# The experts' weight loads wait for a free part of the ring alone, no longer for the load two places before

## The chip, the cores and the metric

The kernel runs on one core of one Trainium2 chip. The metric is the device time of one execution in microseconds, over several executions of the same program; lower is better.

## The reference

Two blocks are computed on 512 tokens of width 1024, in float32. The first is a gated delta rule with a convolution module, followed by a mixture of experts; the second is a diagonal state-space mixer with a convolution, followed by a squared-ReLU MLP. The change touches the mixture of experts alone:

```python
N_EXPERTS = 64; TOP_K = 6; D_EXPERT = 256
scores = jax.nn.sigmoid((hf @ router_w).astype(jnp.float32))
...
_, top_idx = lax.top_k(jnp.where(exp_keep, sel, -jnp.inf), TOP_K)
...
def swiglu(h, wg, wu, wd):
    return (jax.nn.silu(h @ wg) * (h @ wu)) @ wd
def expert_block(args):
    tok, e = args
    return swiglu(h_pad[tok], w_gate[e], w_up[e], w_down[e])
```

Each token goes to 6 of 64 experts. One expert's weights (gate and up 1024 x 256 each, down 256 x 1024) are 3 MB in float32; all 64 are needed in each execution.

## The kernel before, in words

The program is written in a tile framework: each engine has its own stream of instructions, and the framework adds the semaphore waits that the use of tiles demands. Loads are issued by SP (SyncE), whose queue is in order: a transfer that waits holds up all that SP issues behind it.

The experts run as 42 blocks (`BLOCKS`, from `plan`, L1072). Four fixed experts have one block each; the other sixty are ranked by how many tokens they got, and the block of a rank is known when the program is built, while the expert of that rank is read from a table on the chip (`eid`) into a register of SP. A block has up to 128 rows of tokens and belongs to one expert, to two (64 rows each) or to four (32 rows each). Blocks with one expert and blocks with several take turns; the busiest ranks need two blocks, of which the second finds its weights already there.

For each block `blocks` (L1641) does the following. `load_block` asks for the weights: three parts of 1 MB for each expert (part 0 and 1 are gate and up for the first and second half of the 1024 inputs, part 2 is down), all parts 0 first, then all parts 1, then all parts 2. Each part goes into the next slot of a ring (`slot`, L1186): ten slots of their own (`RING`), two more in the memory of `x1` (tag `ewx1`) from the third block on, and in their place three older ones from the 18th block's end on (`free_first`); for the last six blocks (`LEAVE`) ten again. A load must wait until PE has done the last matmul that reads the slot's former content. `rows_ahead` lets POOL (GpSimd) gather the rows of a later block from `hrow` in HBM into one of three tiles X. `ffn` (L1597) turns the rows on PE (`pt_xb`), scales them on DVE and ACT (`xTb`), multiplies by gate and up (`gub`), applies SiLU on ACT (`sgb`) and the product on DVE (`hb`), turns again (`pt_hb`), and multiplies by down (`pyb`) in two halves, which DVE brings into one of three tiles `y`. `scatter` (L1633) lets POOL add the rows to one of two accumulators in HBM (`yacc`), in turn; two scatter-adds on the same accumulator follow one another, each waiting for the one before to land. The gathers and scatter-adds together are called rows below; they go through POOL's DMA queue (q0), the loads through SP's (q1).

In `load` (L1501), the list `order` holds the issued loads. From the third load on, each gets a dependency on the load two places before it (`FLIGHT = 2`, L1061), so that it is issued only when that one has landed. A second, different dependency on `order[-8]` concerns the order of register reads in the program and is no wait for data.

Between the blocks PE also computes the shared expert (`shared`, `shared_out`, at `HID` and `OUT`, behind blocks 10 to 16). Behind block 17 (`SECOND`) the memory of the first stage is given back and SP loads `row_g_final`, `sbc` and `ssd` for the second block. Behind the last expert block, SP issues the first `w_in` loads of the second block, and `beyond` (L1670) waits for all scatter-adds; then `block_two` reads both accumulators (`sums`).

Of the kernel before, what the change touches and what calls it, by code (L numbers as in the profile page):

```python
# [200 lines left out]
class ModWeights:  # L201
# [10 lines left out]
    def load(self):  # L212
        if self.todo:
            j, q = self.todo.pop(0)
            tag, bufs = self.slots[self.n % len(self.slots)]
            self.n += 1
            r = self.rows
            w = self.k.W.tile([P, r, 512], F32, tag=tag, name=f"wm{j}_{q}", bufs=bufs)
            self.k.nc.sync.dma_start(w, self.k.I["w_mod"][j, :, q * r:q * r + r, :])
            self.have.append(w)  # L220
# [837 lines left out]
        50, 49, 46, 45, 44, 44, 43, 42, 41, 41, 40, 39, 38, 37, 37, 32, 32, 32, 31, 30, 30, 28, 26, 25, 23, 22, 20, 20, 18, 17, 16]  # L1058
CAPS = [-(-c // 16) * 16 for c in CAPS]
NOV = 72  # L1060
FLIGHT = 2  # L1061
LEAVE = 6
LAST = 0
AHEAD = 2
# [82 lines left out]
class Moe:  # L1147
# [353 lines left out]
    def load(self, who):  # L1501

        k, nc = self.k, self.k.nc
        if who in self.wt:
            return self.wt[who]
        kind, r = who
        if kind == "rank":
            ins, (v,) = nc.values_load_multi_w_load_instructions(self.eid[:, r:r + 1], engines=[mybir.EngineType.SP],
                                                                 min_val=0, max_val=NE - 1)
            if len(self.order) >= 8:  # L1510
                for q in ins:
                    k.tc.add_manual_dep(q.ins, self.order[-8].ins.name,
                                        mybir.DependencyInfo(mybir.DependencyClass.NoSync, mybir.DependencyReason.DATA),
                                        reason="few registers at a time")
            src = k.I["ew"][bass.ds(v, 1)].rearrange("a p f -> p (a f)")
        else:
            src = k.I["sw"] if kind == "shared" else k.I["ew"][r]
        ts = []

        def part(i):  # L1520
            t = self.slot(f"ew{kind}{r}_{i}")
            q = nc.sync.dma_start(t, src[:, 2048 * i:2048 * i + 2048])
            if len(self.order) >= FLIGHT:
                k.tc.add_manual_dep(q.ins, self.order[-FLIGHT].ins.name,
                                    mybir.DependencyInfo(mybir.DependencyClass.Sync, mybir.DependencyReason.DATA),
                                    reason="few loads in flight, for the rows' sake")
            self.order.append(q)
            ts.append(t)
        self.wt[who] = (ts, part)
        return self.wt[who]  # L1530
# [949 lines left out]
```

## Time and profile before

| | us |
|---|---|
| median of 3 runs (2093.59 to 2098.49) | 2096.74 |
| the profiled execution, its own time | 2084.69 |
| its span, first to last instruction | 2082.9 |
| PE busy | 1853.8 (89%) |
| DVE busy | 994.3 (48%) |
| ACT busy | 596.6 (29%) |
| POOL busy | 501.8 (24%) |

In the profile, times are microseconds (us) from the start of the span unless marked ns. PE is TensorE's matmuls, PEld its weight loads, DVE VectorE, ACT ScalarE, POOL GpSimd, SP SyncE; SPq is SP's queue of issues. L1522 is line 1522 of the kernel; all matmuls stand under one helper's line (L139), so they are told apart by the tile that they write (`gub`, `pyb`, `pt_xb`). A digit of the slices is the busy share in tenths. PEclk is the granted clock of TensorE as a share of full speed. The DMA share is the mean busy share of the core's 16 DMA engines and can pass 1 where packets overlap. A transfer's landing is counted from its issue. An engine's wait is put down to what ended it last.

### The profile page before, as it was taken

To read this page: it belongs to the slowest core of one execution; us is meant where nothing else is said; L and a number is where in the kernel's file an instruction comes from. 1 tells how busy PE (TensorE), PEld (TensorE's weight loads), DVE (VectorE), ACT (ScalarE), POOL (GpSimd) and SP (SyncE) were. 2 spreads that over 40 slices of the span, in tenths; PEclk is the share of its full clock that TensorE was granted. 3 is DMA by queue.
4 is the path that set the end of the run, shared out by engine and by line. 5 is a ranking of instruction groups with operands and counts; after the bars stand their busy time and mean duration, and the time that the engine had idled before them with its cause. 6 is when DMAs were issued, how large, how long until landed. Compare 5 with 4: busy or idle time off the path is not lost. (4 is left out here: it accounts for less than half of the span.)

```text
span 2082.9 us, 24082 instructions
## 1 busy us (share of the span) xinstructions
PE 1853.8 (89%) x8465; PEld 1244.2 (60%) x8465; DVE 994.3 (48%) x2205; ACT 596.6 (29%) x1124; POOL 501.8 (24%) x408
## 2 busy tenths in 40 slices
PE   5997698987798898988888983999999999999998
PEld 3775476875653333333322321888888878888886
DVE  4789944668764211352211215677433453323352
ACT  5443321114332111111111112533333344323341
POOL 1315334533232221212111213543100112201300
PEclk9998888999889999999999997999999999999999
DMA  7354353226589999999999996333332333233241
GB/s 301 134 184 134 95 169 90 74 86 242 188 308 339 348 357 332 338 361 369 351 339 340 367 339 206 105 95 89 101 102 86 101 117 112 89 94 101 81 142 41
DMA packets 136001, 408.53 MB, mean 196 GB/s; under 512 B 43813, under 2 KB 56229, under 8 KB 109513
## 3 DMA queue, kind: packets, MB, share of 16 engines
q1 hardware_dynamic: 110040, 365.17, 49.8%
q0 software_dynamic: 12016, 40.25, 7.7%
q10 hardware_dynamic: 13824, 1.58, 0.5%
q8 instruction: 67, 1.10, 0.2%
q14 instruction: 54, 0.43, 0.1%
HBM read 365.13 MB, written 40.63 MB: 195 GB/s over the span
## 5 line engine op out<-in xcount | busy, mean ns | idle before, releaser
L139 PE MATMUL gub<-ewrank,xTb 128*64 128x512 f32 (+5 forms) x960 | 289.4, 625 | 28.1 <-DMA ewrank<-ew 27.8
L139 PEld LDWEIGHTS gub<-ewrank,xTb 128*64 128x64 f32 (+5 forms) x960 | 94.2, 146 | 199.4 <-issue 156.1
L274 DVE TENSOR_TENSOR wlo<-wraw,whi 128x1024 fp32r<-128x1024 f32 (+1 forms) x103 | 120.8, 1173 | 139.1 <-ACT whi L273 133.7
L273 ACT CAST whi<-wraw 128x1024 fp32r<-128x1024 f32 (+1 forms) x115 | 113.9, 990 | 212.2 <-PE psi L139 50.6
L139 PE MATMUL pyb<-ewrank,hTb 128*64 128x512 f32 (+5 forms) x440 | 155.5, 602 | 5.5 <-DMA ewrank<-ew 3.4
L1616 DVE SCALAR_TENSOR_TENSOR hb<-gub,tw,sgb 128x256 f32<-128x256 f32 (+5 forms) x38 | 18.3, 482 | 274.9 <-ACT sgb L1614 274.9
L139 PE MATMUL psi<-xnh,whi 128*128 128x512 f32 (+1 forms) x368 | 141.7, 386 | 0.0
L139 PE MATMUL psi<-xnl,whi 128*128 128x512 f32 (+1 forms) x368 | 141.4, 384 | 0.0
L1638 POOL DMA_INDIRECT yacc<-yb,tok x63 | 89.0, 1413 | 179.3 <-DVE yb L1630 132.9
L1338 ACT ACTIVATE xTb<-pt_xb,B,A 128x128 f32<-128x128 f32 (+5 forms) x168 | 74.1, 445 | 174.4 <-DVE xTb L1340 173.3
L1593 POOL DMA_INDIRECT X<-hrow,tok x38 | 36.9, 972 | 338.3 <-PE pt_xb L142 332.6
L139 PE MATMUL psi<-xnh,wlo 128*128 128x512 f32 (+1 forms) x296 | 113.3, 383 | 0.0
L1340 DVE TENSOR_SCALAR xTb<-pt_xb,A,B 128x128 f32<-128x128 f32 (+5 forms) x168 | 65.5, 392 | 88.0 <-PE pt_xb L142 51.7
L1614 ACT ACTIVATE sgb<-gub 128x256 f32<-128x256 f32 (+5 forms) x42 | 16.0, 382 | 315.4 <-PE gub L139 315.4
L2403 POOL TENSOR_TENSOR fr<-fr 128x512 f32<-128x512 f32 x32 | 48.7, 1522 | 238.1 <-ACT fr L2402 238.1
L139 PE MATMUL psf<-xml,whi 128*128 128x512 f32 (+1 forms) x272 | 102.5, 377 | 0.2 <-DVE xml L274 0.2
L139 PE MATMUL psf<-xmh,whi 128*128 128x512 f32 (+1 forms) x272 | 102.4, 377 | 0.2 <-ACT xmh L273 0.2
L139 PE MATMUL psf<-xmh,wlo 128*128 128x512 f32 (+1 forms) x272 | 102.4, 377 | 0.0
L139 PEld LDWEIGHTS pyb<-ewrank,hTb 128*64 128x64 f32 (+5 forms) x440 | 46.8, 141 | 78.9 <-issue 64.1
L1630 DVE TENSOR_TENSOR yb<-pyb,gt 128x512 f32<-128x512 f32 (+5 forms) x84 | 57.9, 690 | 71.7 <-PE pyb L139 70.1
L139 PEld LDWEIGHTS psi<-xnh,whi 128*128 128x128 f32 x368 | 69.7, 190 | 14.3 <-ACT xnh L2268 0.4
L139 PEld LDWEIGHTS psi<-xnl,whi 128*128 128x128 f32 x368 | 69.9, 190 | 13.5
(752 smaller groups left out, 4032.6 us busy)
## 6 DMA issues: line engine op xcount, KB each, us to landing
ewrank<-ew SPq DMA_DIRECT2D x168, 1024.0 KB, 7.1
wraw<-w_in SPq DMA_DIRECT2D x59, 512.0 KB, 3.6
wraw<-ff SPq DMA_DIRECT2D x32, 512.0 KB, 3.5
wf<-ff SPq DMA_DIRECT2D x64, 256.0 KB, 2.7
wm<-w_mod SPq DMA_DIRECT2D x28, 512.0 KB, 7.8
ewfix<-ew SPq DMA_DIRECT2D x12, 1024.0 KB, 5.7
ewx<-ew SPq DMA_DIRECT2D x12, 1024.0 KB, 6.9
wm<-w_mod SPq DMA_DIRECT2D x10, 1024.0 KB, 5.7
```

What stands on the lines that cost most here:

```text
L139: return self._done(self.eng.matmul(out, lhsT, rhs, **kw), rate, rhs)
L273: nc.scalar.copy(hi, raw)
L274: (eng or nc.vector).tensor_tensor(lo, raw, hi.bitcast(F32), ALU.subtract)
L1338: nc.scalar.activation(dst(c), pt[:, i, :], AF.Identity, scale=sa, bias=sb)
L1340: nc.vector.tensor_scalar(dst(c), pt[:, i, :], sa, sb, ALU.mult, ALU.add)
L1593: self.k.nc.gpsimd.indirect_dma_start(out=X[0:idx.shape[0]], out_offset=None, in_=self.hrow, in_offset=bass.IndirectOffsetOnAxis(ap=idx, a ...
L1614: nc.scalar.activation(sg[0:n], gu[0:n, 0:256], AF.Silu)
L1616: nc.vector.scalar_tensor_tensor(h[0:n], gu[0:n, 256:512], wslot[0:n], sg[0:n], ALU.mult, ALU.mult)
L1630: nc.vector.tensor_tensor(y[0:n, cs], py[0:n], self.gt2[0:n, cs], ALU.mult)
L1638: self.k.nc.gpsimd.indirect_dma_start(out=self.yacc[self.nsc % 2], out_offset=bass.IndirectOffsetOnAxis(ap=idx, axis=0), in_=y[a:a + n], i ...
L2403: nc.gpsimd.tensor_tensor(r, r, r, ALU.mult)
```

## The change

The constant `FLIGHT` and the dependency on the load two places before are taken out. A load keeps the other conditions: its place in SP's order, its register, and its slot. Nothing else is edited.

```diff
-FLIGHT = 2
 LEAVE = 6
 LAST = 0
 AHEAD = 2
@@ -1520,10 +1519,6 @@
         def part(i):
             t = self.slot(f"ew{kind}{r}_{i}")
             q = nc.sync.dma_start(t, src[:, 2048 * i:2048 * i + 2048])
-            if len(self.order) >= FLIGHT:
-                k.tc.add_manual_dep(q.ins, self.order[-FLIGHT].ins.name,
-                                    mybir.DependencyInfo(mybir.DependencyClass.Sync, mybir.DependencyReason.DATA),
-                                    reason="few loads in flight, for the rows' sake")
             self.order.append(q)
             ts.append(t)
         self.wt[who] = (ts, part)
```

## Rows read from the trace of the kernel before

**Rows 1.** The slices of the page: 40 equal parts of the span, 52 us each.

```profile
DMA  7354353226589999999999996333332333233241
GB/s 301 134 184 134 95 169 90 74 86 242 188 308 339 348 357 332 338 361 369 351 339 340 367 339 206 105 95 89 101 102 86 101 117 112 89 94 101 81 142 41
```

**Rows 2.** The chain that ended last: start us, us, what.

```profile
1270.20 4.86 DMA yacc<-yb,tok
...
1307.38 5.76 PE psi L139 x42
```

**Rows 3.** Waits of SP's queue, 777 to 1262 us: total us, times, longest us.

```profile
SPq L1522 <- DMA ewrank<-ew: 363.7, 128, 8.7
SPq L1522 <- DMA ewx<-ew: 14.5, 5, 3.3
SPq L1522 <- PE gub L139: 3.1, 12, 0.4
```

**Rows 4.** Waits of PE, 777 to 1262 us, same columns.

```profile
PE pt_hb L142 <- DVE hb L1616: 30.3, 29, 1.3
PE gub L139 <- DMA ewrank<-ew: 27.8, 17, 4.2
PE pyb L139 <- DMA ewrank<-ew: 1.9, 3, 1.1
```

**Rows 5.** Windows: PE, PEld, DVE, ACT, POOL busy, then PEclk, DMA share, GB/s.

```profile
8.00:34.00 26.00, 15.61 (x104) 7.73 (x104) 11.21 (x33) 17.30 (x30) 3.09 (x11) 1.00 1.03 420
650.00:777.00 127.00, 116.85 (x497) 45.48 (x499) 31.86 (x78) 20.80 (x51) 30.13 (x24) 1.00 1.00 349
760.00:767.00 7.00, 6.15 (x18) 2.23 (x19) 1.83 (x3) 0.51 (x2) 0.82 (x1) 1.00 0.96 348
777.00:1262.00 485.00, 422.15 (x1467) 154.02 (x1460) 125.62 (x330) 72.84 (x174) 93.01 (x74) 0.96 0.99 348
882.00:887.00 5.00, 3.68 (x13) 1.70 (x12) 3.79 (x13) 1.51 (x4) 0.00 (x0) 1.00 1.04 431
```

**Rows 6.** DMA, 777 to 1262 us: queues, then issues with count and median landing us.

```profile
q1 hardware_dynamic: 20259, 144.47, 78.0%
q0 software_dynamic: 7069, 24.18, 20.4%
...
ewrank<-ew SPq DMA_DIRECT2D x131, 1024.0 KB, 7.2
ewx<-ew SPq DMA_DIRECT2D x4, 1024.0 KB, 6.9
...
yacc<-yb,tok POOLq DMA_INDIRECT x48, 8.3
...
X<-hrow,tok POOLq DMA_INDIRECT x26, 6.9
```

**Rows 7.** Windows, same columns: a wait of PE and what follows.

```profile
1210.00:1215.00 5.00, 1.37 (x6) 0.34 (x6) 0.00 (x0) 0.00 (x0) 0.00 (x0) 0.85 1.01 321
1215.00:1220.00 5.00, 5.00 (x12) 1.30 (x13) 0.00 (x0) 0.00 (x0) 0.00 (x0) 0.50 0.89 316
```

**Rows 8.** Timeline of SP's issues, 0 to 16 us: start us, us, what.

```profile
2.59 2.50 SPq L295 DMA_DIRECT2D xt<-x  x4
5.14 10.02 SPq L219 DMA_DIRECT2D wm<-w_mod  x8
```

**Rows 9.** Timeline of SP's issues, 871 to 878 and 886 to 890 us.

```profile
872.60 0.37 SPq L1824 DMA_DIRECT2D sbc<-sbc  x1
...
874.89 2.65 SPq L1522 DMA_DIRECT2D ewrank<-ew  x2
...
886.80 2.71 SPq L1522 DMA_DIRECT2D ewrank<-ew  x2
```

**Rows 10.** POOL's timeline from 876 us, and the landing of what is issued in 872:878.

```profile
876.45 0.99 POOL L1593 DMA_INDIRECT X<-hrow,tok  x1 [0.32 <-PE pt_xb L142]
...
X<-hrow,tok POOLq DMA_INDIRECT x1, 7.7
```

## The prediction

> **What bounds the kernel now.** I read the slices of the page first, to find the stage that the edited lines feed; then the chain that ended last, to see what a shorter stage is worth; then, for that stage alone, the waits of SP's queue and of PE; then the rates of single stretches and the share of each DMA queue, because they price the change.
>
> The slices [rows 1] show one long stretch, from the 13th slice to the 24th (52 us each, so some 625 to 1250 us), where the DMA digit stands at 9 and the rate at 332 to 369 GB/s. It is the stretch in which `load` (L1501) brings 64 experts of 3 MB each. Behind it the rate falls to about 100 GB/s. The chain [rows 2] leaves this stage by the last scatter-add, issued at 1270.20, and from 1307.38 on it runs through the second block on PE. So whatever the expert stage loses comes off the whole, one for one.
>
> In 777 to 1262 us, the part in which the loads lead, SP waited 363.7 + 14.5 us for the landing of an earlier expert load, and 3.1 us for PE's gate/up to free a slot, never longer than 0.4 us [rows 3]. So the ring had room, and the wait that is to be removed is the one that held the loads back. PE on its side waited 27.8 + 1.9 us for expert weights; another 30.3 us are the step through DVE and ACT between gate/up and down, which no load shortens [rows 4].
>
> **What the two-load limit costs.** The question is whether two loads already keep the DMA engines full. The windows say: nearly, not quite [rows 5]. At 8 to 34 us, where 512 KB loads follow one another without such a limit, the chip moved 420 GB/s at a DMA share of 1.03; at 882 to 887 us, with two expert loads behind a queue of others, 431 at 1.04. At 760 to 767 us only expert loads, two at a time, were under way: 348 GB/s at 0.96. Over 777 to 1262 it was 348 at 0.99, token rows included.
>
> Step 1, a floor for the DMA work of 777 to 1262 us. SP's queue (q1) moved 144.47 MB in it, 135 expert loads (131 + 4) and a few smaller ones [rows 6]. At 420 GB/s that is 344 us. The rows' queue (q0: 48 scatter-adds, 26 gathers) held the engines for 20.4% of the time, 0.204 x 485 = 99 us [rows 6]. The sum is 443 us against 485 that passed: at most 42 us are lost to loads that come too late.
>
> Step 2, the same by the share: 0.99 of 1.03 leaves 4%, 19 us. The two differ because a stalled packet counts as busy: at 760 to 767 the rate was 17% down, the share only 7%. So the loss is 19 to 42 us; I take 30, the middle.
>
> Step 3, can PE follow? Its waits for weights are 29.7 us [rows 4]. Waiting also lowers its clock: at 1210 to 1215 us PE was busy 1.37 of 5 us, and in the next 5 us the granted clock was 0.50, the 1.2 GHz level [rows 7]. Over 777 to 1262 the mean is 0.96 [rows 5], which is half speed for 8% of 485 us, 39 us, in which up to 19 us of work were lost. So PE can give back 30 to 49 us. It doesn't stop a gain of 30, but it is close.
>
> Step 4, before 777 us. In 650 to 777 PE was busy 116.85 of 127 us [rows 5], while it had blocks whose weights were there already and the shared expert. Earlier loads help by 0 to 5 us; I take 2. Before 650 us the slots are held by the first blocks: nothing.
>
> **The change part by part.** *The removed wait*: no instruction goes; each `dma_start` of L1522 from the third on loses one condition. Gain 30 + 2 us by the steps above; bounds 0 (the lost rate has another cause) and 42 + 5 = 47.
>
> *What ends the wait next*: the slot's last reader on PE, or one of SP's DMA semaphores. At the start of the kernel eight transfers of 512 KB took SP 10.02 us to issue, 1.25 us each, after four as large that went out in 2.50 us [rows 8]; that is 420 GB/s, so SP was there held to the pace of landings with several under way. I expect about eight under way, not thirteen. That suffices: it is the state of the 420 GB/s window. Cost: nothing.
>
> *The loads that move earlier past others*: SP's queue is in order. `row_g_final`, `sbc` and `ssd` stand behind the loads of block 17 and need memory that the ring's two extra slots give back, after a matmul of block 16. SP will come to them earlier and may stand there, with the expert loads behind them. Bounds: 0, and one landing, 7.2 us [rows 6]; I take 2, since the loads in front are still coming in then. At the end the first two `w_in` loads come earlier too; the chain there runs over the scatter-add: nothing.
>
> *The rows*: gathers and scatter-adds share the engines with up to eight loads instead of two. A gather is issued when PE has turned the rows of an earlier block and fills a buffer for two or three blocks later (485 us / 26 = 18.7 us a block, so 37 us at least) and takes 6.9 us [rows 6]; the waits of PE [rows 4] have no place for X among the longest. A scatter-add frees one of three `y` and lets the next on the same accumulator start: 24 on each of two in 485 us, one in 20.2 us, landing in 8.3 [rows 6]. How much longer they take behind eight loads is the unknown. The nearest rows are at 872 us, where SP had put `sbc`, its neighbours and two expert loads in the queue [rows 9]. The gather issued at 876.45 landed 7.7 us later, at 884.2 [rows 10]. The load issued before it, at 874.89, landed no earlier than 886.7, because the load that by the code waits for it went out at 886.80 [rows 9]. So a row transfer overtook an older load, and its 7.7 us are close to the median of 6.9. I take 1 to 2 us more per row transfer, hidden; bounds 0, and 7 loads x 2.5 us (1.049 MB at 420 GB/s) = 17.5 us.
>
> On this point the Trainium skill ("DMA: Bandwidth & Descriptors", section Queues, rings and completion order) has a rule: each DMA engine serves the queues that have work in turn, a packet of descriptors at a time. By it the rows' wait wouldn't grow with the number of loads, and the sum would stand as it is; the overtaking at 884 us agrees.
>
> **Sum.** -30 (loads) - 2 (before 777) + 2 (SP's stand at 872) = -30 us. The profiled execution took 2084.69 us with a span of 2082.9, 12 us under the median of 2096.74; the change is taken off the median: 2067 us. With the bounds: -47 to +7, so 2050 to 2104.
>
> **Rivals.**
> 1. *The engines are full already, 0 us.* For it: the share of 0.99, and packets may be slow because loads and rows meet, not because a queue ran dry. Against it: 760 to 767 us at 348 GB/s, with no rows. Time 2093 to 2101. A rule of the Trainium skill speaks for this rival ("DMA: Bandwidth & Descriptors", Specifications): HBM gives a core about 358 GB/s, and 348 is nearly that. The trace differs: this core alone drew 420 over 26 us [rows 5].
> 2. *Only part of the share is won*: 4 to 15 us, 2082 to 2092, if the filled gaps are slowed again by more traffic at once.
> 3. *The rows fall behind the loads: slower.* The mechanism is the two chains of scatter-adds. If a row transfer must let all queued loads pass, it lands 17.5 us later, at 25.8; 24 in a row are 619 us instead of 485, +134. It decides from 20.2 us on, that is with five more loads in front. It limits itself: when PE waits for `y` the ring fills, the loads stop and the rows are quick again. So I price it at +10 to +60, 2107 to 2157. For it: rows and loads share all engines. Against it: the gather at 876.45.
> 4. *It doesn't do what it says*: another wait keeps it at two or three loads. Then nothing moves, 2097; the start of the kernel speaks against it [rows 8].
>
> **How the numbers follow.** The forecast (15 to 47 us less) has 0.58, rival 2 0.08, rivals 1 and 4 together 0.13, rival 3 0.21. About 0.2% (4 us) is what a measurement can tell from no change: faster 0.66, same 0.13, slower 0.21. The predicted time is 2067. The forecast alone spans 2050 to 2082; the range goes from there up to 2105, which takes in rivals 1, 2 and 4 and SP's stand at its worst, and leaves some 0.2 out, nearly all of it rival 3.
>
> **What would show it.** Right: SP's waits of L1522 for expert loads shrink from 378 us to under 100, and waits for PE (slots) or for older transfers come in their place; the median landing of `ewrank` rises from 7.2 to 20 us or more while the rate rises from 348 to some 371 GB/s (348 x 485 us = 168.8 MB, in 455 us); PE's waits for `ewrank` fall under 12 us; the last scatter-add is issued near 1240 instead of 1270, and from there to the end it is 813 us as before; scatter-adds land in 8 to 11 us. Wrong: scatter-adds at 15 us and more, with POOL, DVE or PE waiting for `yacc` or `X`; or a rate that stays at 350 with eight loads under way. What would also make it wrong is an order of SP's or POOL's instructions that the framework lays out differently once the condition is gone; no row of before shows that.

## The result, and the profile after

The changed kernel takes 2037.41 us (median of 4 runs, 2031.66 to 2040.74) against 2096.89 us (median of 4 runs, 2093.59 to 2098.49): a ratio of 0.9725, 95% interval 0.9695 to 0.9754. The gain is 59.5 us, twice the 30 us that were forecast. The profiled execution took 2031.66 us with a span of 2029.9, which is 53.0 us less than the span before. Every engine issues as many instructions as before, but for four semaphore instructions of SP, and SP's transfers and POOL's instructions come in the same order; what was edited is SP's waits. (The load's line has moved up by one, from L1522 to L1521, the lines behind it by five: L1611 is what was L1616.)

The slices, 51 us each, answer to [rows 1]: from the 13th to the 23rd the rate now lies at 334 to 386 GB/s, where it was 332 to 369.

```profile
DMA  8354453227499999999999993333332432333241
GB/s 309 122 186 146 93 158 101 77 73 259 155 343 334 365 384 368 368 375 379 386 382 376 382 333 121 122 94 91 108 99 84 132 102 94 93 94 104 78 140 42
```

The waits of SP's queue, 765 to 1210 us, the same stretch of blocks as [rows 3] (line, releaser, total us, times, longest us):

```profile
SPq L1521 <- DMA ewrank<-ew: 266.2, 109, 4.6
SPq L1521 <- PE gub L139: 28.4, 21, 8.0
...
SPq L1727 <- DMA ewx<-ew: 14.3, 2, 11.8
SPq L1521 <- PE pyb L139: 14.2, 12, 5.1
SPq L1727 <- PE pyb L139: 9.7, 1, 9.7
```

SP still waits for expert loads, but for one eight places before: a load lands after 25.5 us (next fence) and one goes out every 3.3 us (135 in 445), so 7.7 are under way, on average. (The load issued at 1028.88 us, for one, goes out 0.1 us after the eighth before it has landed.) And SP now finds slots in use, 28.4 us for gate/up and 14.2 for down, where it had 3.1 us [rows 3] and 1.8. The DMA queues and transfers of the same stretch, against [rows 6] (queues: packets, MB, share; transfers: count, KB, median us to landing):

```profile
q1 hardware_dynamic: 20160, 143.68, 79.6%
q0 software_dynamic: 7130, 24.38, 21.7%
...
ewrank<-ew SPq DMA_DIRECT2D x131, 1024.0 KB, 25.5
...
yacc<-yb,tok POOLq DMA_INDIRECT x48, 8.3
...
X<-hrow,tok POOLq DMA_INDIRECT x26, 8.7
```

A load takes 25.5 us to land instead of 7.2; the scatter-adds take 8.3 us as before, the gathers 8.7 instead of 6.9. So the rows do not queue behind the loads; at most the gathers lose 1.8 us each, and no wait of PE for `X` stands among the waits below. The Trainium skill ("DMA: Bandwidth & Descriptors", section Queues, rings and completion order) says that a DMA engine serves its queues in turn; these landings agree with it.

PE's waits, 765 to 1210 us, against [rows 4], and the windows, against [rows 5] (PE, PEld, DVE, ACT, POOL busy, then PEclk, DMA share, GB/s):

```profile
PE pt_hb L142 <- DVE hb L1611: 35.4, 29, 6.5
PE pyb L139 <- DMA ewrank<-ew: 4.0, 8, 0.8
PE gub L139 <- DMA ewrank<-ew: 0.5, 3, 0.2
```

```profile
640.00:765.00 125.00, 116.36 (x494) 45.70 (x496) 31.93 (x78) 20.81 (x51) 30.11 (x24) 0.99 1.00 368
765.00:1210.00 445.00, 403.61 (x1472) 152.48 (x1465) 125.72 (x330) 72.83 (x174) 93.19 (x74) 0.99 1.02 378
```

The waits for weights fell from 29.7 to 4.5 us, the rate rose from 348 to 378 GB/s, and the granted clock from 0.96 to 0.99. PE's busy time fell from 422 to 404 us, most of it in the 416 gate/up products of 64 columns, which took 646 ns each before and take 597 now; that fits the half clock that followed a wait [rows 7] and is now rare.

**Where the 53.0 us lie.** Three marks in the timelines of both kernels divide the span: SP's first load of the shared expert, PE's first gate/up of block 13, and the end of the last expert block's down. In the kernel after:

```profile
455.14 0.42 SPq L1521 DMA_DIRECT2D ewshared<-sw  x1
```

```profile
781.47 7.03 PE L139 MATMUL gub<-ewrank,xTb 128*128 128x512 f32 x16
...
1213.01 3.66 PE L139 MATMUL pyb<-ewrank,hTb 128*80 128x512 f32 x8 [0.44 <-ACT hTb L1616]
```

And in the kernel before:

```profile
460.45 0.42 SPq L1522 DMA_DIRECT2D ewshared<-sw  x1
```

```profile
793.03 7.03 PE L139 MATMUL gub<-ewrank,xTb 128*128 128x512 f32 x16
...
1265.54 3.66 PE L139 MATMUL pyb<-ewrank,hTb 128*80 128x512 f32 x8 [0.44 <-ACT hTb L1621]
```

Before, they stood at 460.45, 793.03 and 1269.20 us; now at 455.14, 781.47 and 1216.67. So 5.3 us were gone before any load whose wait was removed; that is a difference between two executions (over all kernels of this document the first mark lies between 453 and 462 us). 6.3 us came between the first and the second mark (1.7 of them ahead of block 3, where kernels without the limit are no faster, see Step 4 below), 41.0 us (476.2 to 435.2) in blocks 13 to 41, and 0.5 us behind them. The change's own share of this pair of executions is some 46 us. The remaining 6.5 us of the 59.5 arise because the profiled execution of before lay 12.2 us under its median, and that of after 5.7 us under its own.

The chain that ended last leaves the stage as it did in [rows 2]: the last scatter-add at 1217.67 instead of 1270.20, 52.5 us earlier, and from there 812 us to the end, as before.

```profile
1217.67 4.83 DMA yacc<-yb,tok
```

### The profile page after: what moved, and what is told of

Its sections match the earlier page's. It is cut to its first block, busy times and chain, and to the rows that moved or that the text cites. A ratio compares the mean times of both kernels' runs of the same rounds, so it can differ in the third digit from the quotient of the medians.

```text
span 2029.9 us, 24078 instructions
## 1 busy us (share of the span) xinstructions
PE 1822.2 (90%) x8465; PEld 1234.0 (61%) x8465; DVE 994.7 (49%) x2205; ACT 596.7 (29%) x1124; POOL 505.9 (25%) x408
## 5 line engine op out<-in xcount | busy, mean ns | idle before, releaser
L139 PE MATMUL gub<-ewrank,xTb 128*64 128x512 f32 (+5 forms) x960 | 268.7, 595 | 0.7 <-DMA ewrank<-ew 0.5
L1611 DVE SCALAR_TENSOR_TENSOR hb<-gub,tw,sgb 128x256 f32<-128x256 f32 (+5 forms) x38 | 18.3, 482 | 232.6 <-ACT sgb L1609 232.6
L1337 ACT ACTIVATE xTb<-pt_xb,B,A 128x128 f32<-128x128 f32 (+5 forms) x168 | 74.1, 445 | 175.4 <-DVE xTb L1339 174.3
```

The lines of the kernel that those rows point to most:

```text
L139: return self._done(self.eng.matmul(out, lhsT, rhs, **kw), rate, rhs)
L1337: nc.scalar.activation(dst(c), pt[:, i, :], AF.Identity, scale=sa, bias=sb)
L1611: nc.vector.scalar_tensor_tensor(h[0:n], gu[0:n, 256:512], wslot[0:n], sg[0:n], ALU.mult, ALU.mult)
```

## The experiments

Theory A: with two loads under way the DMA engines run short, and one or two more would cure it. Its rivals put the gain into the head start of the early loads, into depth as such, or into the token rows.

### How many loads under way

`d3`, `d4` and `d1` are the kernel before with another limit:

```diff
-FLIGHT = 2
+FLIGHT = 3
```

> The limit stands, at three loads under way instead of two; all else as before. Theory A (with two under way the DMA engines run short each time that one lands before the next is issued; a third covers that): nearly all of the gain, 2030 to 2048 us, and 365 GB/s or more from 777 us to the last loads. Theory B (it is the depth that pays: loads far ahead of need, which ride over the bursts of token rows): only a part, 2060 to 2085 us.

> The limit at four. Theory A: the same as with no limit, 2033 to 2042 us. Theory B: between three and no limit, 2045 to 2070 us.

> One load under way; the rest as before. This measures the fixed part of a load: by theory A every load takes 2.5 us of transfer plus issue, start and landing, in all 4.5 to 6 us from one issue to the next, so 131 loads from 777 us on take 590 to 790 us instead of 485, and the kernel 2220 to 2420 us. If the fixed part were so small that two always cover it, the interval would be 2.5 to 3.5 us and the kernel under 2150 us.

Three: 2042.00 us (ratio 0.9733, 0.9674 to 0.9792). Four: 2036.92 us (0.9714, 0.9656 to 0.9772). One: 2437 us, one execution. So the third load brings nearly all, and four are as good as no limit. Depth beyond that buys nothing. In `d3` the loads land after 9.8 us, and the rate from 777 to 1215 us is that of the changed kernel:

```profile
777.00:1215.00 438.00, 395.58 (x1424) 149.82 (x1417) 124.97 (x329) 72.10 (x172) 90.79 (x73) 0.99 1.02 378
```

With one load under way the landing is 5.0 us, rows beside it, and the rate 229 GB/s (720 us from 880 on):

```profile
880.00:1600.00 720.00, 482.66 (x1363) 158.94 (x1364) 124.15 (x323) 71.76 (x169) 89.93 (x71) 0.86 0.72 229
```

```profile
ewrank<-ew SPq DMA_DIRECT2D x128, 1024.0 KB, 5.0
```

At 420 GB/s the 1.049 MB themselves would be 2.5 us; by that estimate, the other half of a load's time moves none of its bytes. The kernel took 17 us more than the top of the expected interval; the granted clock in that window was 0.86.

The Trainium skill has this price ("SBUF — State Buffer", section The DMA setup-cost knee): a transfer takes a fixed 2 us beside its bytes at 436 GB/s. An estimate from this page of the Trainium skill is 4.4 us a load, so that two under way would draw 477 GB/s and suffice; the landing of 5.0 us agrees roughly, the conclusion doesn't, as the next experiment shows.

### Loads alone

`lo2`, `lo3` and `lo0` leave out everything of blocks 13 to 39 but their expert loads (and the work that `hooks` puts behind a block), with two under way, with three, and with no limit.

```diff
             ws = self.load_block(whos)
+            if 13 <= n < 40:
+                while len(Xs) < n + 1:
+                    Xs.append(None)
+                if n in hooks:
+                    hooks[n]()
+                continue
```

> The kernel before, with blocks 13 to 39 cut to their expert loads: no gathers, products or scatter-adds there, two loads under way. Theory A1 (two are too few even for loads alone, as the 348 GB/s of 760 to 767 us says): about 350 GB/s in that stretch, some 125 loads of 1.049 MB in 375 us. Theory A2 (two suffice for loads alone, it is the token rows between them that make the queue run short): 415 GB/s or more, some 315 us.

> The same cut with no limit: about 420 GB/s by both theories, some 312 us for the same loads, since the start of the kernel shows that rate with several loads under way. Less than 400 would say that the floor of the prediction's first step used too high a rate.

> Blocks 13 to 39 cut to their expert loads, as in lo2 and lo0, with three under way. Theory A (the gap between a landing and the first packets of the load that waits for it is the loss; it is covered when two loads, 5 us at 420 GB/s, are left): 415 to 420 GB/s steadily, as without a limit, 1942 to 1946 us. Rival (each load more under way adds rate, up to eight): 380 to 400 GB/s and 1955 to 1975 us.

Windows of `lo2`, then of `lo3`, then of `lo0`:

```profile
860.00:1040.00 180.00, 0.00 (x0) 0.00 (x0) 16.36 (x74) 0.00 (x0) 0.00 (x0) 0.50 0.99 390
1050.00:1170.00 120.00, 19.50 (x60) 5.83 (x61) 3.21 (x7) 2.42 (x6) 0.00 (x0) 0.56 0.85 310
```

```profile
880.00:1090.00 210.00, 0.00 (x0) 0.00 (x0) 0.00 (x0) 0.00 (x0) 0.00 (x0) 0.50 1.01 418
```

```profile
880.00:1090.00 210.00, 0.00 (x0) 0.00 (x0) 0.00 (x0) 0.00 (x0) 0.00 (x0) 0.50 1.01 420
```

With no limit the rate is 420 GB/s for 210 us without a break: the rate that Step 1 of the prediction took from 26 us at the kernel's start holds. Three draw 418. Two draw 390 in one stretch and 310 in another, with no rows beside them. So two are too few for loads alone (A1), and they are at the edge: the same two loads do nearly well for 180 us and badly for the next 120. At 390 GB/s the DMA share is 0.99, almost that of 420 GB/s. How long a load takes to land in the one stretch and in the other:

```profile
ewrank<-ew SPq DMA_DIRECT2D x67, 1024.0 KB, 5.2
...
ewrank<-ew SPq DMA_DIRECT2D x35, 1024.0 KB, 6.9
```

In the first, most issues follow one another after 2.5 to 3.1 us. In the second they come in pairs (1062.86 and 1065.32, 1069.45 and 1071.92, 1076.27 and 1078.72 us): 2.5 us apart, and then some 4.2 us to the next pair. What tips it from one to the other was not found. The times were 1999, 1949 and 1942 us, one execution each.

### Token rows

`nosc2` (two under way) and `nosc0` (no limit) leave out the scatter-adds that come up in blocks 4 to 39; since each is issued a block later, they are those of blocks 3 to 38.

```diff
             while len(pend) > (2 if n < 3 else 1):
+                if 4 <= n < 40:
+                    pend.pop(0)
+                    continue
                 self.scatter(*pend.pop(0))
```

> The kernel before without the scatter-adds of blocks 4 to 39; gathers, products and loads stay, two under way. A1: loads go at some 350 GB/s and lead as before, with gathers alone beside them; 144 MB take 412 us and more, so 2025 to 2045 us with SP still waiting mostly for expert loads. A2: loads run at 400 GB/s or more, PE becomes the bound (422 us busy in the stage): 2020 to 2030 us, with SP waiting for PE to free slots for 100 us or more.

> The changed kernel without the scatter-adds of blocks 4 to 39. If the DMA engines bound the changed kernel (445 us from 765 to 1210 us, of which the rows' queue held them for 97): the stage falls to what PE needs, 15 to 23 us less, 2014 to 2022 us. If PE is already the bound there: 2033 to 2037 us.

`nosc2` took 2038.1 us (ratio 0.9726, 0.9679 to 0.9773) and `nosc0` 2028.87 (0.9682, 0.9642 to 0.9723). The first row below is of `nosc2`, the other fence of `nosc0`, both for 775 to 1205 us:

```profile
SPq L1522 <- DMA ewrank<-ew: 319.6, 126, 5.6
```

```profile
SPq L1521 <- PE gub L139: 127.8, 46, 15.1
SPq L1521 <- PE pyb L139: 117.1, 23, 6.6
SPq L1521 <- DMA ewrank<-ew: 32.3, 19, 5.3
```

In `nosc2` the loads still lead, at 351 GB/s, which PE can just follow; that is A1 again. In `nosc0` they don't lead any more: SP waits 245 us for PE's slots. The gain of `nosc0` on the changed kernel is 8.5 us, less than the 15 to 23 expected: so the loads with the rows beside them set the pace of the changed kernel, but PE follows only some 9 us behind.

### Which loads

`late2` holds loads to two under way from block 13 on, `early2` only before it (its lines read `True` at the start and `n < 13`).

```diff
-            if len(self.order) >= FLIGHT:
+            if self.limit and len(self.order) >= FLIGHT:
...
+            self.limit = n >= 13
             ws = self.load_block(whos)
```

> No limit for the loads of the fixed blocks and of blocks up to 12; two under way from block 13's loads on. Theory A (the rate of the load-bound part from 777 us on carries the gain): 2085 to 2092 us, that is only 5 to 11 us off the kernel before. Rival (the head start carries it: a full ring at 777 us): 2040 to 2055 us.

> Two under way for the fixed blocks and blocks up to 12, no limit from block 13's loads on: the other half of late2. If the two halves add up, and late2 won 6 us: 2040 to 2050 us. If the second half needs the head start of the first: 2050 to 2075 us.

`late2`: 2090.06 us (ratio 0.9963, 0.9930 to 0.9996). `early2`: 2046.59 (0.9733, 0.9682 to 0.9785). Against their own runs of the kernel before (2095.80 and 2101.47) that is 5.7 and 54.9 us; together 60.6, the whole. `late2`'s interval leaves 0.8 to 14.7 us for the early part, and `early2` is 9.2 us above the changed kernel; so it is worth some 6 to 9 us, and the head start carries nothing further.

The profiled execution of `late2` shows something else. Block 13's start and block 41's down:

```profile
787.98 7.03 PE L139 MATMUL gub<-ewrank,xTb 128*128 128x512 f32 x16
...
1275.70 3.66 PE L139 MATMUL pyb<-ewrank,hTb 128*80 128x512 f32 x8 [0.44 <-ACT hTb L1622]
```

From the one to the end of the other it is 491.4 us, with the same limit as before, where the profiled execution of before took 476.2. So at two under way the same stretch differs by 15 us from one execution to the next, and the rate with it: 340 GB/s from 790 to 1210 us against 350. In `early2`, without the limit there, it took 435.1, in the changed kernel 435.2, in `d4` 434.2.

### Bytes or steps

`half4`, `half3` and `half5` cut each load in two of 0.524 MB and allow four, three and five of them. (The order of register reads goes by 16 places instead of 8, that is by as many bytes.)

```diff
-FLIGHT = 2
+FLIGHT = 4
...
-            q = nc.sync.dma_start(t, src[:, 2048 * i:2048 * i + 2048])
...
+            for a in (0, 1024):
+                q = nc.sync.dma_start(t[:, a:a + 1024], src[:, 2048 * i + a:2048 * i + a + 1024])
```

> Each load of 1.049 MB cut into two of 0.524 MB, four of them under way: as many bytes under way as before the change, in smaller steps. Theory A (what is left at a landing has to cover the gap: 1.57 MB here, 1.05 before, 2.10 with three): between the kernel before and d3 and nearer to d3, 2040 to 2065 us. Rival (bytes under way set the rate): as before, 2085 to 2100 us, or slower for the added issues.

> Loads cut in halves of 0.524 MB, three of them under way: 1.57 MB under way, and 1.05 MB left at each landing, as in the kernel before. Theory A (what is left at a landing decides): as before, 2085 to 2105 us. Rival (the bytes under way decide; with four halves, 2.10 MB, it was 2070): 2110 us or more.

> Five halves: 2.62 MB under way, 2.10 MB left at a landing, as with three whole loads. Theory A: as d3, 2037 to 2047 us. Rival (bytes under way, three whole loads being 3.15 MB): between half4 and d3, 2048 to 2060 us; if the added issues of halves cost time of their own, also there.

| under way | MB | median us | GB/s, 790 to 1210 us |
|---|---|---|---|
| 1 whole | 1.05 | 2437.07 | 226 |
| 3 halves | 1.57 | 2176.99 | 301 |
| 2 whole (before) | 2.10 | 2096.89 | 350 |
| 4 halves | 2.10 | 2070.06 | 356 |
| 5 halves | 2.62 | 2047.15 | 369 |
| 3 whole | 3.15 | 2042.00 | 377 |
| 4 whole | 4.19 | 2036.92 | 380 |
| no limit (after) | up to 8 x 1.05 | 2037.41 | 379 |

Theory A had put the loss down to what is left at a landing: 1.05 MB for `half3` as for the kernel before. That fell: `half3` is 80 us slower than the kernel before. Sorted by bytes under way, the times fall without an exception down to four whole loads. At equal bytes, four halves beat two wholes by some 27 us, so the size of the step has a share too, but the smaller one. (Halves also need twice as many issues; what that costs was not measured by itself.) With about 3 MB under way the rate is within 1% of its best.

### SP's stand and a new wait

`ahead` is the changed kernel with nine loads put into SP's queue ahead of `row_g_final` (the upper hunk); `spread` cuts DVE's preparation of the second block into eight steps (the lower hunk; the other steps come up behind blocks 18 to 25); `both` has the two edits.

```diff
+                for f in moe.fixd:
+                    moe.slots.remove(f)
+                for _, _, whos in BLOCKS[18:20]:
+                    moe.load_block(whos)
                 early.close()
-                moe.free_first()
+                moe.slots = moe.first + moe.slots
...
-                Back(ssm_basics(k, k.sb, pool(e1, "ssmt", 1, side="right"))).finish()
+                moe.back = Back(ssm_basics(k, k.sb, pool(e1, "ssmt", 1, side="right")))
+                moe.back.step()
```

> The changed kernel, with the nine loads of blocks 18 and 19 put into SP's queue ahead of row_g_final, sbc and ssd; the two slots in the first block's memory leave the ring before them. If SP's stand there, from 824.8 to 849.3 us, costs what PE waited for weights in block 18 (8 us): 2027 to 2033 us. If the DMA engines alone set the pace and only their dip at 840 to 852 us counts (299 GB/s instead of 378, some 3 us): 2033 to 2036 us. If the stand is hidden: 2037 us.

> The changed kernel, with DVE's preparation of the second block's state space cut into its eight steps, one behind each of blocks 18 to 25, instead of all behind block 17. In the changed kernel PE waited 6.5 us for DVE in block 18. If that wait is on the path: 2031 to 2034 us. If the loads set the pace and absorb it: 2036 to 2038 us.

> The two edits ahead and spread together. If each took away a cost of its own: 2028 to 2032 us. If the loads set the pace in any case: 2034 to 2037 us.

In the changed kernel SP stands before `row_g_final` for 24 us (timeline of its issues):

```profile
820.27 4.89 SPq L1521 DMA_DIRECT2D ewrank<-ew  x3
849.28 0.34 SPq L1727 DMA_DIRECT2D row_g_final<-g_final  x1
```

and the wait that first seemed to follow from it is another one: block 18's second turn waits for DVE, not for a load, while DVE is busy 16.18 of 18 us (PE's timeline, then the window, in which DVE's is the third busy time).

```profile
879.77 0.69 PE L142 MATMUL pt_hb<-cst,hb 128*128 128x128 f32 x2 [6.48 <-DVE hb L1611]
```

```profile
866.00:884.00 18.00, 11.52 (x50) 4.46 (x50) 16.18 (x76) 2.56 (x6) 2.57 (x2) 0.81 1.02 365
```

In the kernel before the longest wait of this kind was 1.3 us [rows 4]. Measured: `ahead` 2034.96 us (2034.05 to 2036.26), `spread` 2036.87 (2030.17 to 2038.70), `both` 2034.87 (2031.61 to 2037.75), the changed kernel 2037.41 (2031.66 to 2040.74). None can be told from the changed kernel, whose own runs span 9 us. By the medians SP's stand costs 2.5 us at most, and it may cost nothing; `ahead` has a wait for DVE of 9.2 us itself. Whether the wait for DVE costs anything is open: in `spread` the longest of this kind still was 6.2 us and in `both` 9.3, so the edit did not take it away.

## Why the prediction was right or wrong

**Right.** The loss was in the rate, and the wait that was removed held it down. What ended the wait next was the transfer eight places before, as named. `ewrank` landed after more than 20 us, and the scatter-adds in 8.3. PE's waits for weights fell under 12 us. The end of the kernel kept its 813 us, to within 1 us. Rival 3 (rows behind loads) did not come: scatter-adds landed as before, gathers 1.8 us later, hidden, as the prediction had it. Rivals 1, 2 and 4 fell with the 59 us. The clock gave back its share, 0.96 to 0.99, as Step 3 allowed. Two signs were missed: SP's waits for expert loads are 266 us instead of under 100, since the limit of eight binds nearly all along (without a loss, as four under way are as fast); and the last scatter-add came at 1217.67 instead of near 1240, which is the size that the next paragraphs account for.

**Wrong: Step 2, and the middle taken from it.** Step 1 gave at most 42 us by rate, Step 2 gave 19 by DMA share, and 30 was taken between them. Blocks 13 to 41 gained 41.0 us: the whole of Step 1. The share was no evidence. The prediction itself said that a stalled packet counts as busy; `lo2` shows how little the share tells, 0.99 at 390 GB/s beside 1.01 at 420 in `lo0`. In its slow stretch, 1050 to 1170 us, the loads kept the engines busy for 2.72 us per MB (84.5% of 120 us for 37.23 MB), in `lo0`, 880 to 1090 us, for 2.41 (101.3% of 210 us for 88.23 MB): fewer bytes under way, and each counts as busy for longer.

```profile
q1 hardware_dynamic: 5105, 37.23, 84.5%
...
q1 hardware_dynamic: 12113, 88.23, 101.3%
```

Rival 2 rested on the same share. Step 1's floor was reached almost: worked out in the same way for the changed kernel (143.68 MB at 420 GB/s, and 21.7% of 445 us for the rows) it is 439 us, and 445 passed. A third and a fourth load are all it takes.

**Too small: Step 4.** Before block 13 the change brought some 5 us, where 2 were taken from bounds of 0 to 5: from PE's first gate/up of block 3 (634.71 us before, 627.76 after) to that of block 13 it is 158.3 us before and 153.7 after; `late2` by its medians has 5.7. One place is block 9's down, where PE waits for weights before and no longer after:

```profile
729.29 3.62 PE L139 MATMUL pyb<-ewrank,hTb 128*32 128x512 f32 x26 [1.51 <-DMA ewrank<-ew]
...
717.69 3.64 PE L139 MATMUL pyb<-ewrank,hTb 128*32 128x512 f32 x32
```

"Before 650 us nothing" stands: `late2` and `nosc0`, which have no limit there, reach block 3 174.2 us after the first mark, the kernel before after 174.3.

**Wrong: the base.** The sum was worked out on a profiled execution that lay 12 us under the median, and then taken off the median. Set against its own execution, the changed kernel is at 2084.7 - 41 - 5 = 2039 us; the median after is 2037. The runs point to that distance as a part of the loss: at two under way the same stretch took 476 us in one execution and 491 in another, while `d4`, `early2` and the changed kernel agree within 1 us; and 13 executions of the kernel before lay between 2082.65 and 2108.23 us, four of `d4` between 2033.86 and 2037.91. So the limit seems to cost more in a typical execution than in the one that was profiled; that this makes up all of the 12 us is not shown.

**The term for SP's stand** (+2) is not visible, and what the medians allow is 2.5 us. Instead there came a wait for DVE that no step had: block 18 now meets DVE's preparation of the second block.

Of the 29.6 us between 2067 and 2037.4, some 11 are Step 2, 3 Step 4, 2 the stand, 7 the difference of the two executions ahead of block 3, and 7 the base.

The rule that spoke for rival 1 (some 358 GB/s for a core) was half read: the Trainium skill says elsewhere ("Perfetto Trace Analysis", section Roofline) that a core whose neighbour is idle can draw more, up to about 120% of it. `lo0` with 420 GB/s, 117% of 358, agrees; what the neighbour did, no run here shows.

## What to carry to other kernels

Compare the rate of a load-bound stretch with the best rate of the same trace, and trust that over the share of busy DMA engines, which falls less than the rate (0.99 at 390 GB/s and 0.85 at 310, beside 1.01 at 420). Hold enough bytes under way: here 1 MB at a time lost 400 us against the changed kernel, 2 MB 60 us and 3 MB 5 us, while scatter-adds on another queue landed as fast with eight loads in front as with two, and gathers 1.8 us later. Where a profiled execution is not the median one, take the change off its own time first, and ask whether the distance to the median is part of what the change removes.

## What the hardware showed unexpectedly

Two loads of 1.049 MB under way, with nothing beside them, drew 390 GB/s for 180 us and then 310 for 120 us in one execution; three drew 418 and some eight 420. And the scatter-adds' median landing was no longer behind some eight loads than beside two: 8.3 us in both kernels.
